# GpSimd's tensor operations in the mixing stages are done by VectorE, in a two-layer decoder trunk

## The chip, the cores and the metric

The kernel runs on one core of a Trainium2 chip. Its engines work side by side, each through its own queue in order: TensorE (PE in the profile) multiplies matrices and writes PSUM; VectorE (DVE) and ScalarE (ACT) work on tiles in SBUF and PSUM; GpSimd (POOL) on tiles in SBUF; SyncE (SP) starts the DMAs that bring the weights. The metric is the device time of one execution in microseconds, lower is better.

## The reference, cut to what matters

The trunk has two layers over 512 tokens of width 1024, all in float32. Each layer is a token mixer with three branches (retention with rotary embedding, HGRN2, a convolution module) and then a gated feed-forward part; both end in a layer norm over a scaled residual.

```python
def _token_mixer(h, positions, lb, w_in, ...):
    p = h @ w_in                                   # one projection for all branches
    rq, rk, rv, rg, gq, gf, gi, gg, ca, cb, gates = split(p)
    q = _rope(heads(rq)); k = _rope(heads(rk)) * 128 ** -0.5
    o = _retention(q, k, heads(rv))                # 4 heads of 128
    u_a = layer_norm_per_head(o) * ret_norm_g * silu(rg)
    logf = logaddexp(log(lb), log1p(-lb) + log_sigmoid(heads(gf)))
    o = _hgrn2(silu(heads(gq)), logf, -expm1(logf), heads(gi))   # 4 heads of 128
    u_b = o * rsqrt(mean(o ** 2) + eps) * hgrn_norm_g * silu(gg)
    u = causal_depthwise_conv(ca * sigmoid(cb), conv_w, conv_b)  # 31 taps, width 512
    u_c = silu(layer_norm(u, conv_ln_g, conv_ln_b))
    g = sigmoid(gates)
    y = g[0] * (u_a @ w_branch[0]) + g[1] * (u_b @ w_branch[1]) + g[2] * (u_c @ w_branch[2])
    return y @ w_out

for l in range(2):
    x = layer_norm(ALPHA * x + g1 * _token_mixer(x * (1 + sc1) + sh1, ...))
    x = layer_norm(ALPHA * x + g2 * _conv_ffn(x * (1 + sc2) + sh2, ...))
```

## The kernel before

Activations lie transposed: 128 channels on the partitions, 512 tokens along the free dimension, so a tile is 128x512. Each weight chunk of 128x1024 is brought by a DMA (`wr`), its high part is made on ScalarE (L216, `wh`) and the remainder on VectorE (L217, `wl`); an activation is split the same way (L229 on ScalarE, L231 on VectorE, in `split`). A product is then three matmuls, L249, L250 and L251 (`mm3`), high by high, high by low, low by high. `proj` makes one 128x512 output from 24 such matmuls and calls `tick` twice, which gives work of two lists its turn: `heads`, the retention and HGRN2 heads in flight, and `fill`, side work in order (rotary tables, the convolution taps of L380 and L383, the convolution's norm, columns of the adaptive modulation of L195 and L196).

A layer's mixer runs in this order. First the convolution inputs; then projections for the heads in the order of `MIX`, with head steps between them; then three gated branches in the order HGRN2, retention, convolution (`ORDER`), each with four rounds: two gate projections (sigmoid on ScalarE, L787), and two branch products that are multiplied by the gate on VectorE (L802) and, from the second branch on, added to the sum so far (L806). In the third branch the finished sum `ys[j]` is split into its two parts, which the output projection reads.

The operations that the change touches, all on GpSimd before:

- L237 in `exact2`: the low part of a tile whose column mean is taken by two matmuls in `colsum` (L243 for the high part, L245 for the low). It serves each head's norm (`head_out`) and the convolution's norm, 20 times.
- L396, L397 and L398 in `conv_norm`: the sum of four tiles, twice a layer, 12 instructions.
- L490 in `hgrn_head`: at each of eight levels the decayed key half `ke` is multiplied by gate products, beside the same for the query half on VectorE (L489); the next level's matmuls (L471, L477) read both. 64 times.
- L532 in `rope`: the swapped half times the sines, between L531 and L533 on VectorE, 16 times.
- L806: the sum of the branches, 32 times.

Nobody wrote an order for the queues by hand: a scheduler walks the program, and places each instruction on its engine by its program position and by when it expects the inputs. A head's matmuls carry an edge to the last projection matmul, so they never run ahead of it. GpSimd keeps some other work in both kernels: products at the start (L723, L725), clearing of head tiles (L455), three subtractions of the last norm (L649) and two output tiles (L693).

Of the kernel before, what the change touches and what calls it, by code (L numbers as in the profile page):

```python
# [10 lines left out]
F32 = mybir.dt.float32  # L11
# [4 lines left out]
ALU = mybir.AluOpType  # L16
# [4 lines left out]
P = 128  # L21
# [68 lines left out]
def trunk(ctx, tc, xT, cT, pos, ada, bada, wts, cols, lbl, rope_c, decay, hmask, outT):  # L90
# [3 lines left out]
    tt = nc.vector.tensor_tensor  # L94
    stt = nc.vector.scalar_tensor_tensor
    ts = nc.vector.tensor_scalar
    ptt = nc.gpsimd.tensor_tensor
# [136 lines left out]
    def exact2(a):  # L234
        hi, lo = big(F32R), big(F32R)
        act(hi, a, AF.Copy)
        ptt(lo, a, hi.bitcast(F32), ALU.subtract)  # L237
        return hi, lo

    def colsum(hi, lo):  # L240
# [152 lines left out]
    def conv_norm(l, acc, out):  # L393
        def total(ts_):
            a, b = big(), big()
            ptt(a, ts_[0], ts_[1], ALU.add)  # L396
            ptt(b, ts_[2], ts_[3], ALU.add)  # L397
            ptt(a, a, b, ALU.add)  # L398
            return a

        a = exact2(total(acc))
        yield 1.5
        yield 1.5
        *_, mu = colsum(*a)
        yield 1.0
        sq = []
        for a in acc:
            stt(a, mu, -2.0, a, ALU.mult, ALU.add)
            s = big()
            act(s, a, AF.Square)  # L410
            sq.append(s)
            yield 0.6
        a = exact2(total(sq))
        yield 1.5
        yield 1.5
        *_, v = colsum(*a)
        yield 1.0
        r = rstd(v, 2.0)
        yield 1.8
        for i, a in enumerate(acc):  # L420
            tt(a, a, r, ALU.mult)
            act(a, a, AF.Silu, bias=col(l, "clb", i), scale=col(l, "clg", i))
            out.append(split(a))
            yield 1.2
# [26 lines left out]
    def hgrn_head(l, h, q, f, ke, sg, v, out):  # L451
# [11 lines left out]
        m, lev = 1, 0  # L463
        while m <= 256:
            z = ps()
            if m == 64 or m == 32:
                for i in range(4):
                    for b in range(64 // m):
                        s0 = 128 * i + 2 * m * b
                        r0 = 2 * m * b  # L470
                        mm(z[r0:r0 + m, m * i:m * (i + 1)], ke[:, s0:s0 + m], qe[:, s0 + m:s0 + 2 * m],  # L471
                           start=True, stop=True)
            elif m < 32:
                for i in range(4):
                    sl = slice(128 * i, 128 * (i + 1))
                    rhs = qe[:, sl].rearrange("p (b two m) -> p b two m", two=2, m=m)[:, :, 1, :]
                    mm(z[:, 64 * i:64 * (i + 1)], ke[:, sl], rhs, start=True, stop=True)  # L477
            elif m == 128:
                mm(z[:, 0:128], ke[:, 0:128], qe[:, 128:256], start=True, stop=True)
                mm(z[:, 128:256], ke[:, 256:384], qe[:, 384:512], start=True, stop=True)  # L480
            else:
                mm(z[:, 0:256], ke[:, 0:128], qe[:, 256:512], start=True, stop=True)
                mm(z[:, 256:512], ke[:, 128:256], qe[:, 256:512], start=True, stop=True)
            if m < 256:
                nb = 256 // m
                qv = qe.rearrange("p (b two m) -> p b two m", two=2, m=m)
                kv = ke.rearrange("p (b two m) -> p b two m", two=2, m=m)
                fv = fm[:, fo:fo + 2 * nb].rearrange("p (b two) -> p b two", two=2)
                tt(qv[:, :, 1, :], qv[:, :, 1, :], fv[:, :, 0:1].broadcast_to([P, nb, m]), ALU.mult)  # L489
                ptt(kv[:, :, 0, :], kv[:, :, 0, :], fv[:, :, 1:2].broadcast_to([P, nb, m]), ALU.mult)  # L490
                if m < 128:
                    fn = 512 - 512 // m
                    tt(F[:, fn:fn + nb], fv[:, :, 0], fv[:, :, 1], ALU.mult)
                    fm, fo = F, fn
            if m == 64 or m == 32:
                pv = pd.rearrange("p (i c) -> p i c", c=128)
                for b in range(64 // m):
                    r0 = 2 * m * b
                    act(pv[r0:r0 + m, :, r0 + m:r0 + 2 * m],
                        z[r0:r0 + m, 0:4 * m].rearrange("p (i c) -> p i c", c=m), AF.Copy)  # L500
            elif m < 32:
                dst = pd.rearrange("p (b two m) -> p b two m", two=2, m=m)[:, :, 1, :]
                nc.vector.copy_predicated(
                    dst, msk[:, 256 * lev:256 * (lev + 1)].rearrange("p (b m) -> p b m", m=m),
                    z[:, 0:256].rearrange("p (b m) -> p b m", m=m))
            elif m == 128:
                act(pf[:, 0:128], z[:, 0:128], AF.Copy)
                act(pg[:, 128:256], z[:, 128:256], AF.Copy)
            else:
                act(pf[:, 128:384], z[:, 0:256], AF.Copy)  # L510
                act(pf[:, 384:512], z[:, 256:384], AF.Copy)
                act(pg[:, 0:128], z[:, 384:512], AF.Copy)
            m, lev = 2 * m, lev + 1
            yield 1.2
# [12 lines left out]
    def rope(q, CC, SS):  # L527
        sw, o = big(), big()
        act(sw[0:64, :], q[64:128, :], AF.Copy)
        act(sw[64:128, :], q[0:64, :], AF.Copy)  # L530
        tt(o, q, CC, ALU.mult)  # L531
        ptt(sw, sw, SS, ALU.mult)  # L532
        tt(o, o, sw, ALU.add)  # L533
        return o

# [177 lines left out]
    for j in range(8):  # L713
# [7 lines left out]
        hi, lo, f = hbuf(), hbuf(), big()  # L721
# [6 lines left out]
    for l in range(L):  # L728
# [20 lines left out]
        for what, h in MIX:  # L749
# [20 lines left out]
            else:  # L770
# [3 lines left out]
                sg = big()  # L774
# [5 lines left out]
        for bi, b in enumerate(ORDER):  # L780
            us = (u_a, u_b, u_c)[b]
            for jp in range(4):
                sg = []
                for t in range(2):
                    q = proj(chunk("in"), hs, TG if bi == 2 else TK)
                    s = big()
                    act(s, q, AF.Sigmoid)  # L787
                    sg.append(s)
                if jp == 0 and bi < 2:
                    while None in us:  # L790
                        for g in heads[:2]:
                            step(heads, g)
                while b == 2 and len(u_c) < 4:
                    step(fill, fill[0])
                w = chunk("br")
                for t in range(2):
                    j = 2 * jp + t
                    q = pm()
                    for k in range(4):
                        mm3(q, sl2(w, 256 * k + 128 * t), us[k], k == 0, k == 3)  # L800
                    tick(1.2)
                    tt(sg[t], q, sg[t], ALU.mult)  # L802
                    if bi == 0:
                        ys[j] = sg[t]
                    else:
                        ptt(ys[j], ys[j], sg[t], ALU.add)  # L806
                    if bi == 2:
                        ys[j] = split(ys[j])

# [194 lines left out]
```

## Time and profile before

| | us |
|---|---|
| median of 3 runs | 1846.57 (1845.42 to 1847.24) |
| the profiled execution's own time | 1846.69 |
| its span, first to last instruction | 1844.9 |
| TensorE busy in it | 1805.0 |
| VectorE busy | 1290.4 |
| ScalarE busy | 751.4 |
| GpSimd busy | 218.8 |
| mean granted TensorE clock | 0.996 |

GpSimd is busy in the mixing stages only (and at the start and the very end), so its share of the span says little; a stage is to be read by itself. Layer 0's heads run until some 310 us, its gated branches until 511 us; layer 1's from 1000 to 1245 and 1424 us. A wait in the rows below is idle time of an engine in front of an instruction, with the instruction that ended it behind the arrow. A busy time of VectorE adds up rows that overlap a little at their ends: where a cost in a queue is wanted, the distance from one start to the next is taken.

### The profile page before, as it was taken

The numbers are of one execution on the slowest core, as the hardware profiler recorded it, in microseconds if no ns is written. First come the engines' busy times: TensorE is split into PE (matmuls) and PEld (weight loads), VectorE is DVE, ScalarE is ACT, GpSimd is POOL, SyncE is SP. The second block draws the span as 40 slices with busy tenths as digits, with TensorE's granted clock in tenths as the row PEclk, the third lists the DMA queues.
The fourth block names the chain that finished last, engine by engine and source line by source line (L and its number), as shares of the span: only waits on it lengthen the run. The fifth ranks groups of instructions, "written<-read, shape, count | busy, mean of one in ns | idle before, by whom it ended". The sixth has DMA issues, their size and how long they took to land.

```text
span 1844.9 us, 23510 instructions
## 1 busy us (share of the span) xinstructions
PE 1805.0 (98%) x9156; PEld 1520.0 (82%) x9156; DVE 1290.4 (70%) x2025; ACT 751.4 (41%) x1042; POOL 218.8 (12%) x187
## 2 busy tenths in 40 slices
PE   7999999999999999999999999999999999999997
PEld 5888877888788888888889987778787988888886
DVE  6995565978869756667489565993775896666344
ACT  3434344333337444432273344453523564444232
POOL 3111231042100000000000221320222000000001
PEclk9999999999999999999999999999999999999999
DMA  8512222226624422255223112222474244222221
GB/s 304 195 70 80 75 75 80 92 103 213 228 73 144 142 103 92 103 183 182 93 90 103 70 69 75 71 76 99 156 245 158 81 142 143 92 103 92 102 82 46
DMA packets 63614, 217.81 MB, mean 118 GB/s; under 512 B 7440, under 2 KB 9872, under 8 KB 63504
## 3 DMA queue, kind: packets, MB, share of 16 engines
q1 hardware_dynamic: 63504, 216.32, 34.2%
q8 instruction: 72, 1.18, 0.3%
q14 instruction: 38, 0.31, 0.1%
HBM read 214.19 MB, written 2.10 MB: 117 GB/s over the span
## 4 chain that ended last, share of the span: by engine, by line
PE 79%; DVE 11%; DMA 4%; ACT 2%; issue 2%; POOL 2%; SPq 0%; DVEq 0%; POOLq 0%; ACTq 0%
PE pm L249 24%; PE pm L251 24%; PE pm L250 24%; DMA ar<-ada 4%; DVE wl L217 2%; DVE ar L195 2%; PE ps L477 2%; DVE b L383 1%; POOL b L806 1%; ACT wh L216 1%; DVE x L655 1%; PE po L552 1%; PE ps L544 1%; DVE b L802 1%; PE ps L250 0%
## 5 line engine op out<-in xcount | busy, mean ns | idle before, releaser
L249 PE MATMUL pm<-h,wh 128*128 128x512 f32 (+1 forms) x1568 | 613.3, 391 | 13.3 <-ACT wh L216 11.6
L251 PE MATMUL pm<-h,wl 128*128 128x512 f32 (+1 forms) x1568 | 603.3, 385 | 0.2
L250 PE MATMUL pm<-h,wh 128*128 128x512 f32 (+1 forms) x1568 | 602.1, 384 | 0.0
L217 DVE TENSOR_TENSOR wl<-wr,wh 128x1024 fp32r<-128x1024 f32 (+1 forms) x301 | 376.8, 1254 | 251.6 <-ACT wh L216 250.5
L216 ACT ACTIVATE wh<-wr 128x1024 fp32r<-128x1024 f32 (+1 forms) x301 | 317.1, 1055 | 490.0 <-PE pm L250 385.2
L249 PEld LDWEIGHTS pm<-h,wh 128*128 128x128 f32 x1568 | 295.6, 188 | 72.0 <-ACT wh L216 11.6
L251 PEld LDWEIGHTS pm<-h,wl 128*128 128x128 f32 x1568 | 295.0, 188 | 61.3 <-DVE wl L217 3.4
L250 PEld LDWEIGHTS pm<-h,wh 128*128 128x128 f32 x1568 | 295.5, 188 | 58.8 <-issue 1.9
L249 PE MATMUL pm<-b,wh 128*128 128x512 f32 (+1 forms) x764 | 280.8, 368 | 6.1 <-ACT b L229 4.7
L250 PE MATMUL pm<-b,wh 128*128 128x512 f32 (+1 forms) x764 | 279.5, 366 | 0.4 <-DVE b L231 0.4
L251 PE MATMUL pm<-b,wl 128*128 128x512 f32 (+1 forms) x764 | 279.1, 365 | 0.0
L383 DVE SCALAR_TENSOR_TENSOR b<-b,cols,b 128x511 f32<-128x511 f32 (+14 forms) x240 | 171.9, 770 | 0.0
L249 PEld LDWEIGHTS pm<-b,wh 128*128 128x128 f32 x764 | 145.0, 190 | 30.5 <-ACT b L229 5.6
L250 PEld LDWEIGHTS pm<-b,wh 128*128 128x128 f32 x764 | 145.0, 190 | 24.5 <-DVE b L231 1.5
L195 DVE SCALAR_TENSOR_TENSOR ar<-ar,cond 128x1024 f32<-128x1024 f32 x96 | 123.5, 1293 | 58.9 <-DMA ar<-ada 58.8
L251 PEld LDWEIGHTS pm<-b,wl 128*128 128x128 f32 x764 | 144.9, 190 | 22.8
L229 ACT ACTIVATE b<-b 128x512 fp32r<-128x512 f32 x88 | 55.4, 630 | 230.7 <-DVE b L852 109.2
L231 DVE TENSOR_TENSOR b<-b,b 128x512 fp32r<-128x512 f32 x88 | 61.1, 694 | 51.9 <-ACT b L229 51.8
L490 POOL TENSOR_TENSOR b<-b,b 128x256 f32<-128x256 f32 x64 | 56.3, 879 | 324.9 <-PE ps L477 218.0
L806 POOL TENSOR_TENSOR b<-b,b 128x512 f32<-128x512 f32 x32 | 57.1, 1784 | 235.2 <-DVE b L802 222.8
L249 PE MATMUL pm<-wh,h 128*128 128x256 f32 x256 | 73.7, 289 | 0.0
L250 PE MATMUL pm<-wl,h 128*128 128x256 f32 x256 | 72.4, 283 | 0.6 <-DVE wl L217 0.6
(222 smaller groups left out, 1899.5 us busy)
## 6 DMA issues: line engine op xcount, KB each, us to landing
wr<-wts SPq DMA_DIRECT2D x299, 512.0 KB, 3.5
ar<-ada SPq DMA_DIRECT2D x96, 512.0 KB, 4.3
x<-xT SPq DMA_DIRECT2D x8, 256.0 KB, 5.8
b<-decay SPq DMA_DIRECT2D x8, 256.0 KB, 3.8
outT<-b SPq DMA_DIRECT2D x16, 128.0 KB, 1.8
b<-hmask SPq DMA_DIRECT2D x3, 256.0 KB, 5.9
cond<-cT SPq DMA_DIRECT2D x1, 512.0 KB, 4.7
wr<-wts SPq DMA_DIRECT2D x2, 256.0 KB, 6.7
```

The lines of the kernel that those rows point to most:

```text
L195: stt(raw, raw, 1.0, cond, ALU.mult, ALU.mult, accum_out=dst)
L216: act(hi[:, s], raw[:, s], AF.Copy)
L217: tt(lo[:, s], raw[:, s], hi.bitcast(F32)[:, s], ALU.subtract)
L229: act(hi, src, AF.Copy)
L231: tt(lo, src, hi.bitcast(F32), ALU.subtract)
L249: mm(dst, a[0], b[0], start=first, stop=False)
L250: mm(dst, a[0], b[1], start=False, stop=False)
L251: last[0] = mm(dst, a[1], b[0], start=False, stop=end)
L383: stt(a[:, d:S], us[i][:, 0:S - d], col(l, "cw", 4 * (CK - 1 - d) + i0 + i), a[:, d:S], ALU.mult, ALU.add)
L477: mm(z[:, 64 * i:64 * (i + 1)], ke[:, sl], rhs, start=True, stop=True)
L490: ptt(kv[:, :, 0, :], kv[:, :, 0, :], fv[:, :, 1:2].broadcast_to([P, nb, m]), ALU.mult)
L806: ptt(ys[j], ys[j], sg[t], ALU.add)
```

## The change

Each of the eight `gpsimd.tensor_tensor` calls of the mixing stages becomes a `vector.tensor_tensor` call with the same operands.

```diff
     def exact2(a):
         hi, lo = big(F32R), big(F32R)
         act(hi, a, AF.Copy)
-        ptt(lo, a, hi.bitcast(F32), ALU.subtract)
+        tt(lo, a, hi.bitcast(F32), ALU.subtract)
         return hi, lo
...
         def total(ts_):
             a, b = big(), big()
-            ptt(a, ts_[0], ts_[1], ALU.add)
-            ptt(b, ts_[2], ts_[3], ALU.add)
-            ptt(a, a, b, ALU.add)
+            tt(a, ts_[0], ts_[1], ALU.add)
+            tt(b, ts_[2], ts_[3], ALU.add)
+            tt(a, a, b, ALU.add)
             return a
...
                 tt(qv[:, :, 1, :], qv[:, :, 1, :], fv[:, :, 0:1].broadcast_to([P, nb, m]), ALU.mult)
-                ptt(kv[:, :, 0, :], kv[:, :, 0, :], fv[:, :, 1:2].broadcast_to([P, nb, m]), ALU.mult)
+                tt(kv[:, :, 0, :], kv[:, :, 0, :], fv[:, :, 1:2].broadcast_to([P, nb, m]), ALU.mult)
...
         tt(o, q, CC, ALU.mult)
-        ptt(sw, sw, SS, ALU.mult)
+        tt(sw, sw, SS, ALU.mult)
         tt(o, o, sw, ALU.add)
...
                     if bi == 0:
                         ys[j] = sg[t]
                     else:
-                        ptt(ys[j], ys[j], sg[t], ALU.add)
+                        tt(ys[j], ys[j], sg[t], ALU.add)
                     if bi == 2:
                         ys[j] = split(ys[j])
```

GpSimd's queue has 192 instructions before and 48 after. The scheduler places the moved ones among VectorE's own and shifts others. At the end of layer 0's third branch, VectorE's queue with the last two sums (`b_2957` and `b_2996` are the sums, `pm` the branch products; + is after):

```order
 L217 TENSOR_TENSOR wl_4094<-wr_4092,wh_4093 128x1024
 L802 TENSOR_TENSOR b_3981<-pm_4026,b_3981 128x512
+L806 TENSOR_TENSOR b_2957<-b_2957,b_3981 128x512
 L231 TENSOR_TENSOR b_4047<-b_2957,b_4045 128x512
 L802 TENSOR_TENSOR b_4018<-pm_4049,b_4018 128x512
+L806 TENSOR_TENSOR b_2996<-b_2996,b_4018 128x512
 L217 TENSOR_TENSOR wl_4126<-wr_4124,wh_4125 128x1024
 L231 TENSOR_TENSOR b_4070<-b_2996,b_4068 128x512
```

Each sum now stands right behind its product, and the second product still behind the low part L231 of the first sum.

In layer 1's convolution norm, VectorE's queue (`b_10520` is the sum of four squares, L237 its low part, `ar` a column of the modulation that a DMA brings):

```order
-L802 TENSOR_TENSOR b_10436<-pm_10462,b_10436 128x512
+L806 TENSOR_TENSOR b_9946<-b_9946,b_10436 128x512
+L396 TENSOR_TENSOR b_10520<-b_10476,b_10479 128x512
+L397 TENSOR_TENSOR b_10521<-b_10503,b_10506 128x512
+L217 TENSOR_TENSOR wl_10533<-wr_10531,wh_10532 128x1024
+L398 TENSOR_TENSOR b_10520<-b_10520,b_10521 128x512
 L195 SCALAR_TENSOR_TENSOR ar_10664,mod_80<-ar_10664,cond 128x1024
-L217 TENSOR_TENSOR wl_10533<-wr_10531,wh_10532 128x1024
-L196 TENSOR_SCALAR mod_80<-mod_80,bad 128x1
+L237 TENSOR_TENSOR b_10526<-b_10520,b_10525 128x512
 L217 TENSOR_TENSOR wl_10575<-wr_10573,wh_10574 128x1024
```

The four operations stand in one row with a weight split, and the low part behind one L195.

In layer 1's fourth HGRN2 head, TensorE's queue (`ps` are the head's level products, `pm_9493` a projection):

```order
 L249 MATMUL pm_9493<-h_7340,wh_9370 128x512
 L250 MATMUL pm_9493<-h_7341,wh_9370 128x512
+L477 MATMUL ps_9420<-b_9314,b_9284 128x64 x4
 L251 MATMUL pm_9493<-h_7340,wl_9371 128x512
 L249 MATMUL pm_9493<-h_7353,wh_9370 128x512
-L477 MATMUL ps_9476<-b_9314,b_9284 128x64 x4
 L250 MATMUL pm_9493<-h_7354,wh_9370 128x512
```

The level `ps_9420` moved here from the projection before, 13 matmuls earlier, and the level `ps_9476` from here into the next projection; from there on the head is some 15 to 20 matmuls later than before, until the projection in which its output is made.

## Rows read from the trace of the kernel before

**Rows 1.** The page, busy time: us, share of the span, instructions.

```profile
PE 1805.0 (98%) x9156; PEld 1520.0 (82%) x9156; DVE 1290.4 (70%) x2025; ACT 751.4 (41%) x1042; POOL 218.8 (12%) x187
```

**Rows 2.** TensorE's waits, 480 to 520 us: total us, times, longest us.

```profile
PE pm L249 <- ACT b L229: 4.7, 2, 2.8
PE pm L249 <- ACT b L787: 1.6, 2, 1.4
```

**Rows 3.** TensorE's waits, 1240 to 1440 us.

```profile
PE pm L249 <- ACT b L787: 1.5, 1, 1.5
PE po L245 <- POOL b L237: 0.9, 1, 0.9
PE po L243 <- ACT b L236: 0.5, 1, 0.5
```

**Rows 4.** TensorE's waits, 1000 to 1240 us.

```profile
PE po L552 <- DVE b L430: 1.2, 1, 1.2
PE ps L544 <- DVE b L546: 1.0, 2, 0.6
PE ps L477 <- DVE b L453: 0.7, 1, 0.7
PE ps L460 <- DVE b L448: 0.5, 1, 0.5
PE po L245 <- POOL b L237: 0.5, 1, 0.5
PE ps L477 <- DVE b L489: 0.4, 1, 0.4
```

**Rows 5.** TensorE's waits, 60 to 480 us.

```profile
PE ps L477 <- POOL b L490: 0.4, 2, 0.2
```

**Rows 6.** Stretches: from:to, length us, busy us (instructions) by engine, clock, DMA, GB/s.

```profile
60.00:310.00 250.00, 249.11 (x1462) 212.97 (x1463) 177.23 (x281) 108.03 (x159) 49.02 (x50) 1.00 0.24 83
...
1130.00:1245.00 115.00, 110.60 (x517) 86.07 (x516) 108.96 (x160) 56.72 (x77) 30.06 (x24) 1.00 0.20 68
...
509.86:516.68 6.82, 5.92 (x13) 4.47 (x14) 2.58 (x3) 1.69 (x2) 0.19 (x1) 0.50 0.37 123
```

**Rows 7.** GpSimd by line, 1130 to 1245 us: count, busy us, mean ns, idle before.

```profile
L237 POOL TENSOR_TENSOR b<-b,b 128x512 fp32r<-128x512 f32 x6 | 9.7, 1610 | 43.0 <-ACT b L236 33.9 <-issue 5.1 <-DVE b L383 4.0
L532 POOL TENSOR_TENSOR b<-b,b 128x512 f32<-128x512 f32 x6 | 8.9, 1476 | 25.6 <-ACT b L530 15.7 <-PE pm L250 9.9
L490 POOL TENSOR_TENSOR b<-b,b 128x256 f32<-128x256 f32 x8 | 7.1, 886 | 21.6 <-PE ps L477 8.6 <-DVE b L493 8.3 <-PE ps L471 1.8
```

**Rows 8.** VectorE in order of time: start us, us, line, operands, idle before.

```profile
1145.52 0.43 DVE L489 TENSOR_TENSOR b<-b,b 128x256 f32<-128x256 f32 x1
...
1156.10 0.69 DVE L533 TENSOR_TENSOR b<-b,b 128x512 f32<-128x512 f32 x1 [1.18 <-POOL b L532]
1156.71 0.68 DVE L309 SCALAR_TENSOR_TENSOR b<-po,b 128x512 f32<-128x512 f32 x1
```

**Rows 9.** VectorE in order of time, tail of layer 0's branches.

```profile
496.83 2.32 DVE L195 SCALAR_TENSOR_TENSOR ar<-ar,cond 128x1024 f32<-128x1024 f32 x1
...
499.81 1.21 DVE L195 SCALAR_TENSOR_TENSOR ar<-ar,cond 128x1024 f32<-128x1024 f32 x1
...
503.72 0.69 DVE L802 TENSOR_TENSOR b<-pm,b 128x512 f32<-128x512 f32 x1
```

**Rows 10.** GpSimd in order of time, same stretch.

```profile
495.93 2.14 POOL L806 TENSOR_TENSOR b<-b,b 128x512 f32<-128x512 f32 x1 [2.13 <-DVE b L802]
...
507.94 2.10 POOL L806 TENSOR_TENSOR b<-b,b 128x512 f32<-128x512 f32 x1 [2.13 <-DVE b L802]
```

**Rows 11.** VectorE's taps by line: in 1130 to 1245 us; the widest shape in the whole span.

```profile
L383 DVE SCALAR_TENSOR_TENSOR b<-b,cols,b 128x511 f32<-128x511 f32 (+29 forms) x60 | 47.2, 830 | 0.0
...
L383 DVE SCALAR_TENSOR_TENSOR b<-b,cols,b 128x511 f32<-128x511 f32 x8 | 5.6, 745 | 0.0
```

**Rows 12.** ScalarE in order of time, tail of layer 0's branches.

```profile
505.84 0.63 ACT L229 ACTIVATE b<-b 128x512 fp32r<-128x512 f32 x1 [3.90 <-POOL b L806]
...
510.08 0.63 ACT L229 ACTIVATE b<-b 128x512 fp32r<-128x512 f32 x1 [2.66 <-POOL b L806]
```

## The prediction

> **What bounds the kernel now.** The first view is the busy time of each engine: TensorE is busy for 1805.0 of the 1844.9 us span [rows 1]. So the change can give only what TensorE waits, and it can take only by making TensorE wait more. The second view is TensorE's waits, stretch by stretch. From 480 to 520 us, where the last gated branch of layer 0 ends and the output projection begins, it idles 4.7 us in two waits for the high part of a merged tile (L229, the longest 2.8 us) and 1.6 us for gate sigmoids (L787) [rows 2]. From 1240 to 1440 us, in the gated branches of layer 1, it is 1.5 us for a sigmoid and 0.9 and 0.5 us for the two parts of a convolution sum [rows 3]. From 1000 to 1240 us, the heads of layer 1, the six waits are 1.2, 1.0, 0.7, 0.5, 0.5 and 0.4 us, together 4.3 us [rows 4]. In the heads of layer 0, 0.4 us are for the key product of L490 [rows 5]. The third view is the table by stretch: from 509.86 us on, behind the waits of layer 0's tail, TensorE's granted clock is 0.50, that is 1.2 instead of 2.4 GHz, for 6.82 us [rows 6]; at half speed it does 3.4 us of work there, so it loses 3.4 us. The same table shows VectorE busy for 108.96 of 115 us from 1130 to 1245 us, that is full, and for 177.23 of 250 us in layer 0's heads [rows 6]. All the waits named and the clock are 4.7 + 1.6 + 3.4 + 1.5 + 0.9 + 0.5 + 4.3 + 0.4 = 17.3 us: the most that I can see the change give.
>
> **What it removes, and what the same work costs on VectorE.** 144 GpSimd instructions go: 64 key products of 128x256 and 80 operations of 128x512 (32 branch sums, 20 low parts, 16 rotary products, 12 convolution sums). In the full stretch of layer 1 GpSimd takes 1610 ns for a low part, 1476 ns for a rotary product and 886 ns for a key product [rows 7]. On VectorE a 128x512 product or sum of two tiles takes 0.69 us, and the next instruction starts 0.61 us after it (1156.10 to 1156.71); a key product has a twin in L489, which takes 0.43 us [rows 8]. So every step gets shorter, to half or less. VectorE gets 80 x 0.61 + 64 x 0.43 = 76 us more, nearly all of it in some 600 us of mixing stages.
>
> **What VectorE gets back.** VectorE's rows are longer where a GpSimd tensor operation runs beside them. The 1024-wide product L195 takes 2.32 us at 496.83, and 1.21 us at 499.81 with GpSimd idle [rows 9]; the branch sum on GpSimd that lies beside the first starts at 495.93 and takes 2.14 us [rows 10], so it ends at 498.07, some 1.1 us into the product, and 1.11 us is what the product lost. From 1130 to 1245 us the 60 convolution taps L383 take 830 ns in the mean against 745 ns for their widest shape undisturbed [rows 11]: at least 60 x 0.085 = 5.1 us lost in this line alone. The narrower taps should take less, and other lines are lengthened too, so I estimate 10 us in all, double that. VectorE also waited 1.18 us for a rotary product of GpSimd before 1156.10 [rows 8]. In this stretch GpSimd ran 6 low parts, 6 rotary products and 8 key products [rows 7], with 3 convolution sums: 15 x 0.61 + 8 x 0.43 = 12.6 us are added to VectorE. Net: from +7.5 us (only L383's 5.1 us come back) to about +1 us (10 us and the 1.18 us come back). I take +1 us, because the row at 496.83 is the nearest, and what it lost ended with the GpSimd instruction.
>
> The Trainium skill says why in "SBUF — State Buffer", section "Who interferes with whom": GpSimd's SBUF port is also VectorE's second one, and whichever comes later stands still until the other's instruction is over. By that rule all the lengthened rows go back to their short form, as taken above; if it did not hold, the stretch would come out at the +7.5 us end. The row at 496.83, 1.11 us longer, agrees.
>
> **The tail of layer 0** [rows 9, 10, 12]. Before, the last two merged tiles go through L802 on VectorE (503.72), the sum on GpSimd and the high part on ScalarE; the last high part starts at 510.08, since its sum starts at 507.94 and takes 2.10 us. After, as the order shows, VectorE does L802, L806, L231, L802, L806 in a row. From 503.72, with steps of 0.61 us: the first sum starts at 504.33, its high part runs from 504.95 to 505.58 (0.63 us), L231 waits for it and ends at 506.2, the second L802 at 506.8, the second sum at 507.45, and the last high part starts there instead of at 510.08. That is **2.6 us** on the path, for TensorE's 2.8 us wait ends on this high part. What is late next is the weight split before 503.72, which the change does not touch. TensorE's two waits for high parts shrink with it: the first high part ended at 506.47 and now does at 505.58, so the first wait falls from 4.7 - 2.8 = 1.9 us to 1.0; the second ends 2.6 us earlier but begins 0.9 us earlier, so it falls from 2.8 to 1.1. With the 1.6 us for sigmoids, at most unchanged, it idles 3.7 us instead of 6.3. A single wait of 1.5 us later on [rows 3] is followed by no slow stretch. I take it that the clock stays up: **3.4 us**, with 0 as the other end.
>
> **Layer 1's gated branches** [rows 3]. The convolution sum had to queue behind two branch sums on GpSimd. On VectorE it is three steps of 0.61 us with one weight split (about 1.2 us) among them and some 3 us earlier, which covers the waits of 0.9 and 0.5 us: **1.4 us**. In the new order L195, which needs a DMA, stands just ahead of the low part L237; in the trace of before it ran at that place without a wait, so I price that at nothing; without that cover a DMA wait would stand on this path, and all of the 1.4 us could go. The 1.5 us wait for a sigmoid stands behind a high part on ScalarE, which waits for a branch sum like the one of 2.14 us; 1.5 us earlier, it is gone: **1.5 us**.
>
> **The heads** [rows 4, 5]. The waits on L448, L453, L489 and L237 (0.5 + 0.7 + 0.4 + 0.5 us) follow rows of VectorE or GpSimd that were lengthened; I take them as gone, and of the other 2.2 us (L430 and L546, queued behind taps) 0.4 us: **2.5 us**. TensorE's order shifts too: the fourth HGRN head's matmuls stand later among the projections, which gives VectorE time. In layer 0: **0.4 us**.
>
> **What it adds.** The 20 low parts and the sums now stand in VectorE's queue, and a low part waits there for ScalarE's high part, some 0.55 us each time; taps, weight splits and the next level of a head are queued behind it. In the full stretch that is 6 x 0.55 = 3.3 us, which TensorE feels only when a head is late: between 0 and 3.3 us. I charge **1.2 us**. On SP's queue only two decay loads move, each by one place; they lead their use by most of a head and are priced at nothing.
>
> Sum: 2.6 + 3.4 + 1.4 + 1.5 + 2.5 + 0.4 - 1.2 = 10.6 us. The profiled execution took 1846.69 us, 1.8 us beyond its span; the median of the runs is 1846.57 us, so one number serves for both: 1846.7 - 10.6 = **1836.1 us**.
>
> **The rivals.**
> (a) *The clock falls all the same and the heads give nothing*: 10.6 - 3.4 - 2.5 = 4.7 us, 1842.0 us. For it: TensorE still idles 3.7 us of some 9 in the tail, and its new order has never run. Against: the longest wait there more than halves.
> (b) *A wash*: VectorE's queue takes what the tails give. If the net load of layer 1's heads is at the 7.5 us end, and the 3.3 us of low-part waits pass on to TensorE in full, 1846.7 - 11.8 + 7.5 + 3.3 = 1845.7 us. Against: the projections run on while a head is late.
> (c) *Slower: VectorE becomes the bound of layer 1's heads.* The place is 1130 to 1245 us, with 6.0 us free on VectorE. If the lengthened rows keep their length, all 12.6 us are added to a full engine, TensorE's fixed order passes each on, and the heads' gain of 2.9 us is gone: 1846.7 - 8.9 + 1.2 + 12.6 = 1851.6 us. The old time is passed once TensorE loses more than 8.9 - 1.2 = 7.7 us there, which needs VectorE to get back less than 4.9 of the 12.6 us. Against: the L383 rows alone show 5.1. The Trainium skill speaks for this rival in "Perfetto Trace Analysis", section "Optimizing Scalar/DVE Operations": where VectorE is saturated, moving work off it, even to GpSimd, may pay, and this change undoes such a move where VectorE is full. The page itself adds that between these two engines it might not help, and the trace bears out that addition.
>
> **How the numbers follow.** Forecast 0.55; (a) 0.23; (b) 0.13; (c) 0.09. A measurement of this kernel can tell about 0.2%, 3.7 us, from no change. Faster: the forecast and four fifths of (a), 0.73. Same: the rest of (a) and (b), 0.18. Slower: (c), 0.09. The range begins at 1829.0, where all 17.3 us are given, and ends at 1846.5, beyond (a) and (b); outside lie (c) and a few per cent below, some 1 in 8.
>
> **What would show it.** Right: no L195 or L217 row at twice its length in the mixing stages; the last high part of layer 0's merge within 4.5 us of the first L802 of its pair; no stretch at clock 0.50 near 500 us; no wait of TensorE on L236, L237 or L787 after 1240 us; VectorE's busy time in the heads of layer 1 within a few us of 109. Wrong: VectorE near 115 of 115 us there and TensorE's waits on L489, L490 or L546 above 4.3 us, or new waits for the weight splits.

## The result and the profile after

| | us |
|---|---|
| changed kernel, median of 4 runs | 1823.85 (1823.17 to 1824.75) |
| kernel before, median of 4 runs beside it | 1846.9 (1845.42 to 1848.14) |
| ratio | 0.9876, interval 0.9859 to 0.9893 |
| span of the profiled execution | 1821.9 (before 1844.9) |

The changed kernel is faster by 23.0 us, more than the 17.3 us that the prediction took for the most that the change could give, and outside its range. The busy times of the page, beside [rows 1]:

```profile
PE 1796.9 (99%) x9156; PEld 1519.2 (83%) x9156; DVE 1314.0 (72%) x2169; ACT 752.9 (41%) x1042; POOL 35.4 (2%) x43
```

TensorE's idle time, span less busy, falls from 1844.9 - 1805.0 = 39.9 us to 1821.9 - 1796.9 = 25.0 us, by 14.9 us; the other 8.1 us of the gain are "busy" time of the same 9156 matmuls. VectorE is busy for 23.6 us more than before and the kernel is shorter all the same, so the load of VectorE as a whole says nothing. By stretch (columns as in [rows 6]; the first two of the changed kernel, the last of the kernel before):

```profile
1130.00:1245.00 115.00, 114.83 (x544) 91.98 (x544) 107.29 (x175) 55.12 (x75) 0.00 (x0) 1.00 0.23 81
470.00:515.00 45.00, 45.00 (x200) 37.24 (x199) 32.08 (x57) 14.73 (x19) 0.00 (x0) 1.00 0.56 187
```

```profile
470.00:515.00 45.00, 38.45 (x155) 29.87 (x154) 36.35 (x58) 13.64 (x18) 10.32 (x6) 0.94 0.59 202
```

The tail of layer 0 has TensorE at 45.00 of 45 us, at clock 1.00, where it had 38.45 us at 0.94. VectorE is not fuller there but emptier, 32.08 against 36.35 us. From 1130 to 1245 us TensorE does 544 matmuls instead of 517 and VectorE's busy time is 1.7 us below the 108.96 of [rows 6]. Of the waits in [rows 2 to 5] none is left: the same view shows nothing from 60 to 520 us and from 1240 to 1440 us, and this one row from 1000 to 1240 us:

```profile
PE ps L482 <- ACT b L508: 0.2, 1, 0.2
```

To see where 23 us come from, I took for every matmul the time to the start of the next one, less the median of its kind, and compared the two kernels place by place. The difference is 10.9 us in the tail of layer 0 (480 to 520 us; the slow clock is in it), 5.9 us in the heads of layer 1, 4.0 us in its gated branches, 1.5 us in the heads of layer 0. That is 22.3 of the 23.0 us. A second way is to count the matmuls of both kernels off in queue order and to compare when the same place is reached. It gives 11.0, 6.3, 4.1 and 1.3 us, together 22.6 us. Where a difference is said below to be "by queue order", it was read in this second way.

### The profile page after: what moved, and what is told of

Its sections match the earlier page's. It is cut to its first block, busy times and chain, and to the rows that moved or that the text cites. A ratio compares the mean times of both kernels' runs of the same rounds, so it can differ in the third digit from the quotient of the medians.

```text
span 1821.9 us, 23388 instructions
## 1 busy us (share of the span) xinstructions
PE 1796.9 (99%) x9156; PEld 1519.2 (83%) x9156; DVE 1314.0 (72%) x2169; ACT 752.9 (41%) x1042; POOL 35.4 (2%) x43
## 4 chain that ended last, share of the span: by engine, by line
PE 93%; DVE 4%; ACT 1%; DMA 1%; issue 0%; SPq 0%; DVEq 0%; ACTq 0%
PE pm L249 28%; PE pm L251 28%; PE pm L250 28%; PE ps L477 2%; PE ps L544 1%; PE po L552 1%; DVE wl L217 1%; DVE ar L195 1%; DVE x L655 1%; DMA ar<-ada 1%; ACT wh L216 1%; PE ps L471 0%; PE ps L460 0%; PE ps L250 0%; DVE h L679 0%; PE ps L251 0%
## 5 line engine op out<-in xcount | busy, mean ns | idle before, releaser
L249 PE MATMUL pm<-h,wh 128*128 128x512 f32 (+1 forms) x1568 | 611.6, 390 | 11.2 <-ACT wh L216 11.2
L217 DVE TENSOR_TENSOR wl<-wr,wh 128x1024 fp32r<-128x1024 f32 (+1 forms) x301 | 367.3, 1222 | 244.1 <-ACT wh L216 243.3
L249 PEld LDWEIGHTS pm<-h,wh 128*128 128x128 f32 x1568 | 295.5, 188 | 69.7 <-ACT wh L216 11.2
L383 DVE SCALAR_TENSOR_TENSOR b<-b,cols,b 128x511 f32<-128x511 f32 (+14 forms) x240 | 162.5, 730 | 0.0
L195 DVE SCALAR_TENSOR_TENSOR ar<-ar,cond 128x1024 f32<-128x1024 f32 x96 | 116.7, 1221 | 47.5 <-DMA ar<-ada 46.9
L231 DVE TENSOR_TENSOR b<-b,b 128x512 fp32r<-128x512 f32 x88 | 60.6, 689 | 32.0 <-ACT b L229 32.0
L249 PE MATMUL pm<-wh,h 128*128 128x256 f32 x256 | 73.6, 288 | 0.0
L251 PE MATMUL pm<-wh,h 128*128 128x256 f32 x256 | 72.2, 283 | 0.0
L847 DVE SCALAR_TENSOR_TENSOR b<-pm,cols,b 128x510 f32<-128x510 f32 x84 | 62.5, 748 | 2.2
```

What stands on the lines that cost most here:

```text
L195: stt(raw, raw, 1.0, cond, ALU.mult, ALU.mult, accum_out=dst)
L217: tt(lo[:, s], raw[:, s], hi.bitcast(F32)[:, s], ALU.subtract)
L231: tt(lo, src, hi.bitcast(F32), ALU.subtract)
L249: mm(dst, a[0], b[0], start=first, stop=False)
L251: last[0] = mm(dst, a[1], b[0], start=False, stop=end)
L383: stt(a[:, d:S], us[i][:, 0:S - d], col(l, "cw", 4 * (CK - 1 - d) + i0 + i), a[:, d:S], ALU.mult, ALU.add)
```

## The experiments

The two theories: **A**, a moved operation matters by its own time on the path that TensorE waits for (the prediction's sum was mostly this); **B**, it matters because VectorE stands still beside a GpSimd operation, so that its queue comes late where TensorE needs it. All kernels compute the whole reference. "Gain" is the difference of medians to the kernel before on the same chip. The medians of the kernel before go from 1845.32 to 1846.9 us over the chips, so a run is set against the changed kernel by the two gains, 23.0 us less its own, and not by the bare medians.

| kernel | median us | ratio to before, interval | gain us |
|---|---|---|---|
| sums of L806 alone | 1831.96 | 0.9919 (0.9904 to 0.9934) | 14.6 |
| heads alone (L237, L490, L532) | 1838.10 | 0.9951 (0.9936 to 0.9966) | 8.5 |
| convolution sums alone | 1843.43 | 0.9989 (0.9980 to 0.9999) | 2.6 |
| last two sums of layer 0 alone | 1845.07 | 0.9991 (0.9982 to 1.0001) | 1.5 |
| sums of the third branch alone | 1836.87 | 0.9949 (0.9932 to 0.9965) | 9.4 |
| changed, GpSimd busy beside all | 1857.40 | 1.0053 (1.0038 to 1.0068) | -10.8 |
| changed, GpSimd busy beside the sums | 1834.83 | 0.9939 (0.9925 to 0.9954) | 11.2 |
| changed, GpSimd busy in the heads | 1844.41 | 0.9989 (0.9980 to 0.9998) | 1.9 |
| changed, longer path at the sums | 1824.19 | 0.9880 (0.9866 to 0.9895) | 21.9 |
| changed, longer path in the heads | 1824.78 | 0.9885 (0.9871 to 0.9900) | 21.5 |
| the same at the sums, order held | 1826.27 | 0.9894 (0.9877 to 0.9910) | 19.1 |
| nothing but clears and casts on GpSimd | 1825.56 | 0.9889 (0.9874 to 0.9904) | 20.5 |

### The parts one at a time

The sums alone: of the diff, only L806.

```diff
-                        ptt(ys[j], ys[j], sg[t], ALU.add)
+                        tt(ys[j], ys[j], sg[t], ALU.add)
```

> Only the 32 branch sums of L806 go to VectorE; TensorE's order is that of the kernel before. Theory A (the path: what counts is the sum's own 2.1 us on the way to a high part): the prediction's terms of the branches, 2.6 + 3.4 + 1.5 = 7.5 us, so 1839.4 us, and some 3.7 us of waits stay in layer 0's tail. Theory B (the queue: VectorE came to the tail late, because its L195, L661, L662 and L217 rows stood still beside GpSimd's sums and because it waited for the high parts behind them): all waits and the slow clock of layer 0's tail go, 10.9 us, and the 1.7 us at 1384 and 0.4 us at 482, so 13.0 us and 1833.9 us.

Measured 1831.96 us, 14.6 us of gain: B's number (13.0 us) and more. No wait of TensorE is left from 480 to 520 us and the clock there is 1.00; the 1.5 us at a sigmoid of layer 1 is gone, and of the two waits for the convolution sum, whose GpSimd operations no longer queue behind branch sums, one of 0.2 us is left. By queue order 11.0 us come in the tail of layer 0 and 3.7 us in layer 1's gated branches.

The heads alone: L237, L490 and L532 are VectorE's, the rest is GpSimd's; TensorE's order is that of the changed kernel.

```diff
-        ptt(lo, a, hi.bitcast(F32), ALU.subtract)
+        tt(lo, a, hi.bitcast(F32), ALU.subtract)
...
-                ptt(kv[:, :, 0, :], kv[:, :, 0, :], fv[:, :, 1:2].broadcast_to([P, nb, m]), ALU.mult)
+                tt(kv[:, :, 0, :], kv[:, :, 0, :], fv[:, :, 1:2].broadcast_to([P, nb, m]), ALU.mult)
...
-        ptt(sw, sw, SS, ALU.mult)
+        tt(sw, sw, SS, ALU.mult)
```

> Only the heads' operations (L490, L532) and the low parts L237 go to VectorE; TensorE's order is that of the changed kernel. Theory A (the prediction's terms): 2.5 + 0.4 - 1.2 = 1.7 us, and some of the wait at 1309, so 1844 to 1845 us. Theory B (VectorE's rows in the heads stood still beside GpSimd, 30 us of the 51 in the trace, and come back to their short form): the steps of TensorE in the heads lose 5.9 + 1.5 us fewer, 7.4 us, and at most 0.9 us at 1309, so 1838.5 to 1839.5 us.

Measured 1838.1 us, 8.5 us: B's number. From 1000 to 1240 us TensorE waits 0.2 us instead of 4.3. The two parts add up to 23.1 us, the whole gain, though the convolution sums are in neither.

The convolution sums alone (L396 to L398):

```diff
-            ptt(a, ts_[0], ts_[1], ALU.add)
-            ptt(b, ts_[2], ts_[3], ALU.add)
-            ptt(a, a, b, ALU.add)
+            tt(a, ts_[0], ts_[1], ALU.add)
+            tt(b, ts_[2], ts_[3], ALU.add)
+            tt(a, a, b, ALU.add)
```

> Only the 12 sums of the convolution's norm (L396 to L398) go to VectorE; TensorE's order is that of the kernel before. The prediction's term: the waits of 0.5 and 0.9 us at 1309 us go, 1.4 us, so 1845.3 us. By the queue (theory B), these waits came from sums queued behind branch sums on GpSimd, and most of them goes too, 1.0 to 1.8 us: 1845 us. Both within what can be told from no change; what decides is the waits in the trace.

Measured 1843.43 us, 2.6 us of gain; the interval just excludes no change. In the trace the waits for L236 and L237 after 1240 us are gone and the 1.5 us at the sigmoid stays, as the prediction's term of 1.4 us says. By queue order 1.9 us come there, and 2.0 us more in the tail of layer 0, where the listed waits for sigmoids fall from 1.6 to 0.4 us; no convolution sum stands there (the last one of layer 0 starts at 409.69 us before), and why these waits shrink was not tested.

### How far the last pair reaches

The last two sums, at the place for which the prediction has its largest terms:

```diff
-                        ptt(ys[j], ys[j], sg[t], ALU.add)
+                        (tt if bi == 2 and jp == 3 and l == 0 else ptt)(ys[j], ys[j], sg[t], ALU.add)
```

> Only the last two sums of layer 0's third branch go to VectorE. Theory A (the prediction's own chain of the tail): the wait of 2.8 us falls by 2.6 us, and the clock stays at 1.00: 6.0 us, 1840.7 us; or, if the clock falls all the same, 2.6 us, 1844.1 us. Theory B agrees on that, and says that VectorE's first product of the pair still starts at about 503.7 us, so the wait for a sigmoid (1.4 us) and the first wait for a high part (1.0 us or more) stay. If the whole 10.9 us come (1836 us), the earlier sums play no part and B falls.

Measured 1845.07 us, 1.5 us, with no change inside the interval: less than either number expected (6.0 or 2.6 us). VectorE's and ScalarE's rows of this kernel (start us, us, line, operands, idle before):

```profile
507.54 0.68 DVE L802 TENSOR_TENSOR b<-pm,b 128x512 f32<-128x512 f32 x1
508.26 0.69 DVE L806 TENSOR_TENSOR b<-b,b 128x512 f32<-128x512 f32 x1
...
511.70 0.63 ACT L229 ACTIVATE b<-b 128x512 fp32r<-128x512 f32 x1 [1.14 <-DVE b L806]
```

From the first product to the last high part it is now 4.16 us, against 6.36 us in [rows 9, 12]: the chain got 2.2 us shorter, near the 2.6 us predicted. TensorE's waits are still there, and so is the slow clock, though for a shorter time: the mean of 0.54 over the 3.70 us below stands for some 3.4 us at 0.50, where before it was 6.82 us.

```profile
509.67 0.49 PE L249 MATMUL pm<-b,wh 128*128 128x512 f32 x1 [1.23 <-ACT b L229]
...
512.38 0.49 PE L249 MATMUL pm<-b,wh 128*128 128x512 f32 x1 [1.25 <-ACT b L229]
```

```profile
513.20:516.90 3.70, 3.44 (x9) 2.72 (x9) 2.14 (x3) 1.06 (x1) 0.00 (x0) 0.54 0.38 142
```

About 1 us was also lost at another wait for a sigmoid, 1.31 us before 485.32 where the same wait was 0.26 us before the change. So the last pair by itself doesn't carry the tail.

The eight sums of the third branch in each layer:

```diff
-                        ptt(ys[j], ys[j], sg[t], ALU.add)
+                        (tt if bi == 2 else ptt)(ys[j], ys[j], sg[t], ALU.add)
```

> Only the 16 sums of the third branch (eight in each layer) go to VectorE; the 16 of the second branch stay on GpSimd. TensorE's order is that of the kernel before. Theory A (path of the last pair): as with the last two sums, 1845 us, and up to 1.6 us less for layer 1's sigmoid: 1843.5 us. Theory B (VectorE's queue through the whole third branch): the tail's 10.9 us and the sigmoid's 1.7 us go, 1834 us, near the 1832.0 us of all 32 sums.

Measured 1836.87 us, 9.4 us: between the two, and nearer to B. By queue order 8.5 of the 11.0 us of the tail are in it. It shows where the tail was lost. The products L802 of layer 0's third branch start so long after the last matmul of their product (the matmuls counted off in queue order), in us, for the four pairs:

| | 1 | 2 | 3 | 4 |
|---|---|---|---|---|
| before | 7.0, 7.9 | 10.8, 11.5 | 12.4, 13.2 | 7.6, 8.3 |
| last two sums alone | 7.3, 9.0 | 12.1, 12.8 | 14.4, 14.9 | 8.3, 7.6 |
| third branch alone | 6.6, 6.9 | 7.1, 7.0 | 8.8, 10.6 | 3.9, 3.9 |
| changed | 1.7, 2.0 | 2.5, 2.4 | 4.2, 6.4 | 0.0, 0.0 |
| changed, GpSimd busy beside the sums | 5.5, 7.6 | 9.3, 9.1 | 13.4, 15.2 | 8.6, 7.5 |

VectorE was already 7 us late when the third branch began, fell back further in it, and stood 7.6 us behind at the last pair, where TensorE has no other work in its queue. With the third branch's sums moved 3.9 us are left, with all sums none. In the third-branch kernel TensorE still waits twice in the tail, 1.3 and 0.6 us, without a stretch at half clock.

### Standing still or path: one without the other

GpSimd busy beside each moved operation, but nobody waiting for it: the changed kernel with an operation of the same shape on GpSimd whose result nobody reads. The queues of TensorE, VectorE, ScalarE and SyncE are in the changed kernel's order, row by row.

```diff
-        tt(lo, a, hi.bitcast(F32), ALU.subtract)
+        tt(lo, a, hi.bitcast(F32), ALU.subtract); ptt(a, a, cond[:, 0:512], ALU.subtract)
...
-                        tt(ys[j], ys[j], sg[t], ALU.add)
+                        tt(ys[j], ys[j], sg[t], ALU.add); ptt(sg[t], sg[t], cond[:, 0:512], ALU.add)
```

(and in the same way behind L398, three times, L490, into a tile of its own, and L533)

> The changed kernel, and beside each moved operation GpSimd does one of the same shape on operands that are not needed any more, with results that nobody reads. The orders of TensorE, VectorE, ScalarE and SyncE are those of the changed kernel. Theory A (the path): nobody waits for these operations, so the time is the changed kernel's, 1823.9 us, within 1 us. Theory B (VectorE stands still beside GpSimd): some 50 us of VectorE's rows are lengthened again, and what the prediction missed, some 12 us, or more goes again: 1834 to 1840 us.

Measured 1857.40 us: 10.8 us slower than the kernel before, so 33.8 us of gain are gone. A, by which the time would not move, fails. B has the direction, but its size is missed: it gave 10 to 16 us. In the trace no idle time of TensorE, VectorE or ScalarE ends on one of these operations. ScalarE, at 751.6 us, is as busy as in the changed kernel (752.9 us), and VectorE is busy for 1381.0 instead of 1314.0 us with the same 2169 instructions. VectorE's rows from the tail of layer 0 of this kernel, and then GpSimd's of the same stretch:

```profile
504.00 1.21 DVE L195 SCALAR_TENSOR_TENSOR ar<-ar,cond 128x1024 f32<-128x1024 f32 x1
...
505.14 1.74 DVE L231 TENSOR_TENSOR b<-b,b 128x512 fp32r<-128x512 f32 x1
```

```profile
498.63 1.29 POOL L806 TENSOR_TENSOR b<-b,cond 128x512 f32<-128x512 f32 x1 [15.13 <-DVE gbt L662]
504.10 2.24 POOL L806 TENSOR_TENSOR b<-b,cond 128x512 f32<-128x512 f32 x1 [4.17 <-DVE mod L196]
```

GpSimd's sum starts 0.10 us after VectorE's L195 and takes 2.24 us where the one at 498.63 takes 1.29: it gets going only as L195 ends. L231 then starts beside it and takes 1.74 us instead of 0.69; it ends 0.54 us after GpSimd's row, so it did little before. The rule of the Trainium skill in "SBUF — State Buffer", section "Who interferes with whom", that the later of the two stands still until the other's instruction is over, is what these rows show, in both directions.

The same at the sums alone (of the edit above, only the line behind L806), and in the heads alone (only those behind L237, L490 and L533):

> The changed kernel, and after each of the 32 branch sums GpSimd adds a constant tile to the gate product, which nobody needs any more; nobody waits for the result. All other queues have the changed kernel's order. Theory A (a sum costs by its time on the path): 1823.9 us, within 1 us. Theory B (a GpSimd operation makes VectorE stand still): VectorE's rows beside the 32 operations are lengthened by some 20 us, and layer 0's tail comes late again, so 8 to 15 us of the 23 go: 1832 to 1839 us.

> The changed kernel, and beside each key product (L490), rotary product (L532) and low part (L237) GpSimd does an operation of the same shape on operands that are not needed any more; nobody waits for the results, and all other queues have the changed kernel's order. Theory A (path): 1823.9 us, within 1 us. Theory B (VectorE stands still): VectorE's rows in the heads are lengthened by 40 us or more, and TensorE waits for level products again: with 33.5 us for all dummies together and 11.0 us for those at the branch sums, 18 to 22 us, so 1842 to 1846 us.

Measured 1834.83 and 1844.41 us, which is 11.8 and 21.2 us of gain gone: B in both, 33.0 of the 33.8 us together. In the first, TensorE's waits of the tail are back, and VectorE's low part L231 is what got longest there (440 to 515 us; the first row is of this kernel, the second of the changed one):

```profile
L231 DVE TENSOR_TENSOR b<-b,b 128x512 fp32r<-128x512 f32 x8 | 9.3, 1159 | 0.7 <-ACT b L229 0.7
```

```profile
L231 DVE TENSOR_TENSOR b<-b,b 128x512 fp32r<-128x512 f32 x9 | 6.2, 687 | 0.7 <-ACT b L229 0.7
```

By queue order the tail of layer 0 loses some 12 us against the changed kernel, all that the change had given there and 1.0 us more; half clock for 6.82 us from 508.95 us on is in it. Layer 1's gated branches lose only 0.5 of their 4.1 us, although VectorE's rows are lengthened there too. So B is enough for the tail and not for layer 1's gated branches, where the prediction's own account, shorter sums on the way to the waits, is left.

In the second TensorE waits for level products in both layers' heads; from 1000 to 1240 us (total us, times, longest):

```profile
PE ps L477 <- DVE b L490: 3.1, 3, 1.8
PE ps L544 <- DVE b L546: 2.6, 3, 1.7
```

These 21.2 us are well over twice the 8.5 us that the heads alone gave. VectorE does the moved work here and stands still as well, and twice, behind waits of 1.66 and 1.78 us, TensorE's clock is at 0.50 for 3.4 us, which costs 1.7 us each time. So the run shows what standing still can cost in the heads; it does not measure its share in the kernel before.

The other way round, a longer path with GpSimd idle. ScalarE copies each sum in place twice, some 1.2 us that the high part has to wait:

```diff
-                        tt(ys[j], ys[j], sg[t], ALU.add)
+                        tt(ys[j], ys[j], sg[t], ALU.add); act(ys[j], ys[j], AF.Copy); act(ys[j], ys[j], AF.Copy)
```

> The changed kernel, and after each of the 32 branch sums ScalarE copies the sum in place twice, about 1.2 us more before the high part can start, which is what a sum on GpSimd took longer, but with GpSimd idle. TensorE's order is the changed kernel's, and VectorE's differs by a few places about the sums. Theory A (path): the 7.5 us that the prediction gave to shorter sums go again, 1831 us or more. Theory B (VectorE's queue): the tails wait some 1 us longer at most, 1823.9 to 1826 us.

Measured 1824.19 us, 1.2 us of gain gone, where A had the time at 1831 us or more. And in the heads, one copy behind L237, L490 and L532:

```diff
-        tt(sw, sw, SS, ALU.mult)
+        tt(sw, sw, SS, ALU.mult); act(sw, sw, AF.Copy)
```

> The changed kernel, and after each key product, rotary product and low part of the heads ScalarE copies the result in place: the path gets some 0.5 us longer each time, about what GpSimd took longer than VectorE with nothing beside it, while GpSimd is idle. TensorE's order shifts by some dozens of places in the heads. Theory A (path): the heads' gain goes, 8 us, so 1832 us. Theory B (VectorE stands still): 1824 to 1828 us.

Measured 1824.78 us, 1.5 us of gain gone, where A had 1832 us. Neither is told apart from the changed kernel: the intervals of the ratios overlap. TensorE's order in the heads is another here, so the shift of the fourth head isn't what made the gain either. Against this, the scheduler saw the copies and put VectorE's low parts L231 later, which may have hidden the path. So the last run of this kind holds each product L802 behind the low part of the sum before it, as it stands in both kernels:

```diff
-                    tt(sg[t], q, sg[t], ALU.mult)
+                    with tc.issue_after(low[0].ins): tt(sg[t], q, sg[t], ALU.mult)
```

(`low[0]` is the last L231; the two copies stay)

> The run with two ScalarE copies behind every branch sum, and VectorE's products L802 held behind the low part L231 of the sum before, as in the kernel before and the changed kernel; so the order cannot hide the longer path, and GpSimd stays idle. Before, VectorE stood idle in front of L231 for the high part for 7.0 us (440 to 515 us) and 15.6 us (1340 to 1425 us); changed, 0.7 and 2.1 us; with the two copies and a free order, 0.5 and 1.1 us. Theory C (an in-order wait: part of the gain of the sums is that VectorE no longer waits at L231): these waits come back, about 1.2 us each for 16 low parts, and 3 to 8 us of the 14.7 us of the branch sums go, 1827 to 1832 us. Theory B alone (VectorE stands still beside GpSimd): 1824 to 1825.5 us.

Measured 1826.27 us: 0.7 us below C's times and 0.8 us above B's. The gain is 4.0 us less than the changed kernel's, inside C's loss of 3 to 8 us, but the intervals overlap, so the total decides nothing. By queue order the profiled execution loses 1.7 us in the first 60 us, where no branch sum runs, and 1.0 us at the sums: 0.4 us in the tail of layer 0 and 0.6 us in layer 1's gated branches. That is the price of the longer path here. But the run doesn't bring back what it was to bring back. VectorE in front of the low part L231 from 440 to 515 us and from 1340 to 1425 us, first before, then in this run (count, busy us, mean ns, idle before):

```profile
L231 DVE TENSOR_TENSOR b<-b,b 128x512 fp32r<-128x512 f32 x8 | 5.5, 688 | 7.0 <-ACT b L229 7.0
...
L231 DVE TENSOR_TENSOR b<-b,b 128x512 fp32r<-128x512 f32 x8 | 5.5, 693 | 15.6 <-ACT b L229 15.6
```

```profile
L231 DVE TENSOR_TENSOR b<-b,b 128x512 fp32r<-128x512 f32 x9 | 6.2, 686 | 2.0 <-ACT b L229 2.0
```

Before, VectorE stood idle there for 22.6 us, here for 2.0 + 2.0 (the row reads the same in both stretches). So the runs show that standing still is enough by itself to take 11.8 us at the sums, and that 1.2 us more of path takes some 1 us in the trace. How much of the 14.6 us each of the two took in the kernel before, where VectorE both stood still and waited at L231, stays open.

### Taking the rest off GpSimd

```diff
-        nc.gpsimd.memset(pd, 0.0)
+        nc.vector.memset(pd, 0.0)
...
-                    ptt(x, x, zs, ALU.subtract)
+                    tt(x, x, zs, ALU.subtract)
```

(likewise `pts` to `ts` in L693, L723 and L725)

> The changed kernel, with GpSimd's other tensor work moved to VectorE too: the products at the start (L723, L725), the clearing of head tiles (L455), three subtractions of the last norm (L649) and two output tiles (L693). Theory B: VectorE's last lengthened rows, 1.9 us, get short, but 8 x (0.69 + 0.69) us and 8 clears are added to it, and the last norm waits for 3 more subtractions on VectorE: 1821 to 1827 us, no change that can be told. Theory A: 8 products of 2.0 us at the start leave the path of the residual, which nobody waits for: 1824 us.

Measured 1825.56 us, a gain of 20.5 us: nothing is added to the 23.0 us. VectorE gets 11.4 us more work and there were only 1.9 us of lengthened rows left to win. No run gained more than the changed kernel.

## Why the prediction was wrong, by its steps

**What bounds the kernel: right, but measured too small.** TensorE did bound it. The step that failed is "All the waits named and the clock are ... 17.3 us: the most that I can see the change give". The waits were added up as the view lists them, as idle time after a matmul's modelled end, and some rows of the same views were left out. These two go with the change as well, the first from 60 to 480 us, the second once in each of the stretches of [rows 2] and [rows 3], together 0.9 us:

```profile
PE ps L471 <- DVE b L493: 0.5, 1, 0.5
PE pm L250 <- DVE b L231: 0.2, 1, 0.2
```

More is lost in what a row doesn't show. Before, at the wait in the tail:

```profile
498.47 0.39 PE L251 MATMUL pm<-b,wl 128*128 128x512 f32 x1
500.22 0.50 PE L249 MATMUL pm<-b,wh 128*128 128x512 f32 x1 [1.36 <-ACT b L787]
```

From start to start it is 1.75 us where the step from one such matmul to the next is otherwise 0.23, so 1.52 us are lost, and the row says 1.36: the end of a matmul of 0.39 us covers the first 0.16 us of such a wait, and a shorter wait isn't listed. By starts, the difference in the four places is 22.3 us, where the rows and the clock had 17.3 us. The range began at the 17.3 us (1846.7 - 17.3 is 1829.4; it says 1829.0) and so missed the time by 5.2 us.

**Each operation is shorter on VectorE: right.** The moved sum takes 0.69 us (508.26 above).

**What VectorE gets back: right, and too little was made of it.** Set against the short rows of their own line and shape, some 93 rows of VectorE beside GpSimd had lost 51.0 us before, 9 rows 1.9 us after; so of the 76 us of moved work VectorE's busy time shows only 23.6 us more. From 1130 to 1245 us the lost time was 11.8 us, near the estimate of 10 us. (The sum on GpSimd ends 1.24 us into the L195 of 496.83, not 1.1 us; that changes nothing.) The prediction worked this out for one stretch and never for the tail. In the heads of layer 1 (1000 to 1245 us, before and after) the query product, a neighbour of the moved key product, shows it:

```profile
L489 DVE TENSOR_TENSOR b<-b,b 128x256 f32<-128x256 f32 x32 | 16.2, 506 | 24.4 <-PE ps L477 14.2 <-PE ps L471 6.4 <-PE ps L480 3.7
```

```profile
L489 DVE TENSOR_TENSOR b<-b,b 128x256 f32<-128x256 f32 x32 | 13.6, 424 | 23.0 <-PE ps L477 13.2 <-PE ps L471 6.2 <-PE ps L480 3.5
```

**The tail of layer 0: 2.6 + 3.4 us predicted, 10.9 us measured.** The step that failed is "What is late next is the weight split before 503.72, which the change does not touch". The split stood in a queue that was 7.6 us late, and the change touches what made it late: the waits at L231 (7.0 us before and 0.7 us after, from 440 to 515 us) and the rows beside the branch sums, L195 above all. L195 also waits for its DMA there, but about as long after as before (the first row is of before):

```profile
L195 DVE SCALAR_TENSOR_TENSOR ar<-ar,cond 128x1024 f32<-128x1024 f32 x18 | 26.1, 1456 | 7.2 <-DMA ar<-ada 7.2
```

```profile
L195 DVE SCALAR_TENSOR_TENSOR ar<-ar,cond 128x1024 f32<-128x1024 f32 x16 | 19.5, 1222 | 8.2 <-DMA ar<-ada 8.2
```

After, VectorE waits for TensorE at this place:

```profile
494.00 0.69 DVE L802 TENSOR_TENSOR b<-pm,b 128x512 f32<-128x512 f32 x1 [0.31 <-PE pm L251]
494.73 0.69 DVE L806 TENSOR_TENSOR b<-b,b 128x512 f32<-128x512 f32 x1
...
498.17 0.64 ACT L229 ACTIVATE b<-b 128x512 fp32r<-128x512 f32 x1 [0.57 <-DVE b L806]
```

The chain itself was right: 4.17 us from the first product to the last high part (3.73 predicted, within the 4.5 named), and the run with only the last two sums shortened it by 2.2 us. The rest that the prediction left standing, 3.7 us with the 1.6 us for sigmoids "at most unchanged", went with the lateness. The sigmoid of layer 1 had been taken as gone; that those of the tail would stay was given no reason.

**The clock: 3.4 us came, not for the reason given.** The prediction had waits left at the tail and the clock staying up; no wait was left. In the last-two run the two high-part waits had shrunk about as the prediction wanted (1.23 and 1.25 us, 1.0 and 1.1 us predicted), and the clock fell all the same, for some 3.4 us: rival (a)'s half of the story was right for the change that the prediction had described. With the 1.3 and 0.6 us of the third-branch run it stayed up.

**Layer 1's gated branches: 2.9 us predicted, 4.0 us measured.** The waits of both terms went, and each is larger by starts than as listed. The record fits the mechanism: with GpSimd busy beside the sums and nobody waiting for it, 3.6 of the 4.1 us by queue order stay.

**The heads: 2.5 + 0.4 - 1.2 = 1.7 us predicted, 5.9 + 1.5 = 7.4 us measured**, 8.5 us with the heads alone. All six waits went, L430 and L546 among them, of which the prediction took 0.4 of 2.2 us. L430 stood behind four taps that took 3.74 us from 1181.36 on, with a low part on GpSimd beside them; in front of L546 the nearest rows are short, and what made it late lies further back and isn't shown. The charge of 1.2 us for low parts that wait in VectorE's queue isn't seen: one 0.2 us wait is left, and with a ScalarE copy behind every such operation the heads lose 0.3 us by queue order.

**The rivals.** None happened. What (c) named as its condition, lengthened rows that keep their length under the added work, is what the run with GpSimd busy beside all makes true: 10.8 us slower than before, against 4.9 us for (c), which counted one stretch only. The rule of the Trainium skill in "Perfetto Trace Analysis", section "Optimizing Scalar/DVE Operations", that moving work off a full VectorE may pay, isn't borne out here: with VectorE at 108.96 of 115 us, the opposite move gained 23.0 us. The signs that the prediction named for being right all came (the last high part 4.17 us after its pair's first product, VectorE at 107.29 us in the heads, no wait on L236, L237 or L787 after 1240 us); none of them tells 10.6 us from 23.0 us.

## What to carry to other kernels

Before crediting GpSimd with relief of VectorE, look for VectorE rows at double their usual length beside it, and set what they lose (51.0 us here) against the work it took over (some 76 us): here GpSimd relieved VectorE of some 25 us, and TensorE paid 23.0 us for it. Find how late an in-order engine is where its work is due, product by product, and not only what it is doing when TensorE finally waits: the last item in the queue is not what is late. Size the most that a change can give from the starts of the matmuls, not from the listed waits.

## What the runs showed of the hardware that I had not expected

A GpSimd operation whose result nobody wants is far from free: 144 of them cost 33.8 us, with VectorE's rows 67 us longer. The standing still goes both ways: the same GpSimd sum took 1.26 to 2.34 us in the kernel before. And TensorE's granted clock is hard to foretell from waits: two of 1.3 and 0.6 us close together left it at 1.00, five of 0.4, 1.4, 1.2, 0.2 and 1.3 us (the last-two run) were followed by a stretch at half clock. One and the same wait of 1.66 us for a key product in layer 0 left it at 1.00 with GpSimd busy beside all, at 110.59 us, and was followed by 3.4 us at half clock with GpSimd busy in the heads, at 110.79 us.
